# A delta-net decoder step on one core: the substitution on 16x16 blocks instead of 32x32

## The chip, the core and the metric

The kernel runs on one NeuronCore of a Trainium2 chip. Five engines work side by side, each through its own queue in order: TensorE (PE, matmuls), VectorE (DVE), ScalarE (ACT), GpSimd (POOL) and SyncE (SP), which here issues all DMAs. They wait for each other by semaphores. An engine that waits holds up everything behind it in its own queue. The metric is the device time of one execution in microseconds; below it is the median of several runs.

## The reference

Two layers, each with four mixers on the same normalised input; the change is in the first of them, the gated delta net. There are 272 prompt positions (16 learned ones and 256 tokens) and 8 sequences of 4 new tokens, 304 columns in all. The recurrence is computed in chunks, and each chunk needs a unit lower triangular system solved:

```python
def step(s, inp):
    qc, kc, vc, bc, gc = inp
    gcum = jnp.moveaxis(jnp.cumsum(gc, axis=1), 1, 2)
    decay = jnp.exp(jnp.where(incl, gcum[..., :, None] - gcum[..., None, :], -jnp.inf))
    kb = kc * bc[..., None]
    a = jnp.where(strict, jnp.einsum('bihk,bjhk->bhij', kb, kc) * decay, 0.0)
    rhs = jnp.concatenate([jnp.moveaxis(vc * bc[..., None], 1, 2),
                           jnp.moveaxis(kb, 1, 2) * jnp.exp(gcum)[..., None]], axis=-1)
    sol = lax.linalg.triangular_solve(a + eye, rhs, left_side=True, lower=True)
    u, w = sol[..., :dv], sol[..., dv:]
    v_new = u - jnp.einsum('bhik,bhkv->bhiv', w, s)
    ...
```

Around the mixers stand one input projection and one output projection per layer; these are most of the arithmetic:

```python
proj = jnp.einsum('bld,de->ble', rms_norm(x, lp['norm']), lp['w_in']).astype(f32)
...
y = x + jnp.einsum('ble,ed->bld', mixed.astype(x.dtype), lp['w_out'])
```

## The kernel before

**The main stream.** The loop at the end of `trunk` runs over units: layer, phase ("in" or "out"), output tile of 128 columns, and a quarter of the 2048 inputs. A unit is four weight blocks of 128x128 and three matmuls for each: the input as a high and a low part (`xh`, `xl`) against the weights' high part (`hi`), and the high input against the weights' low part (`lo`). Weights come by DMA into `raw`, ScalarE makes `hi`, VectorE makes `lo`, some units ahead of PE. This stream writes the tile `main` in PSUM (and `d` for the first units). In all there are 6144 of these matmuls in the order, 128x304 or a little narrower.

**The background threads.** The mixers are Python generators that a planner interleaves with the main stream while the program is built. After each weight block the loop calls `bg.poll()`; a thread gets its next stretch, up to its next `yield`, when the planner's clocks say that what it waits for is done by PE's clock. The clocks are kept in `Clocks.op`, with a price per operation in `price`. The resulting order is fixed when the program is built: each engine's queue is what the planner wrote. In each layer three thread groups run beside the in-phase: the delta net (`delta_thread`, one head pair after the other, PSUM tag `d`), a chain of row sums and the GLA pairs, and the RG-LRU and retention pairs (both tag `e`). The out-phase starts when all gated results (`m`) are there.

**The delta net's inverse.** For a pair of heads there are 2 heads and up to 10 diagonal blocks of 32x32 a head. `delta_thread` writes them to DRAM (`dk`), and reads them back so that a block lies in one partition's row: 20 blocks, four times over, on 80 partitions. Each copy r solves for 8 of the block's 32 right-hand columns. POOL then runs a forward substitution, one step per row j:

```python
for j in range(31):
    n, m = 31 - j, j // 4 + 1
    ...
    pool.tensor_mul(tv, bk[:, j:j + 1, j + 1:32].to_broadcast([80, m, n]), ...)
    pool.tensor_sub(xk[:, 0:m, j + 1:32], xk[:, 0:m, j + 1:32], tv)
```

The work tiles lie in the big buffers called `s9`. The inverses go through DRAM again (`dx`) into one tile `XB`; VectorE transposes it in blocks of 32, POOL copies the blocks into wide tiles `UF`, and PE joins 32 to 64 and 64 to 128 by small matmuls with the off-diagonal blocks of `BM` (the decayed k k^T). The results then solve for the chunk's values and states. In the profile the names `n`, `m` and `g` are shared work buffers, `hq` and `lq` are the high and low part of a square whose sum over partitions PE forms with `onesr`, `zk` and `zq` belong to the GLA pairs, `lso` to the RG-LRU, and `ssq` is the sum of squares for the norm. All of these calls go through one wrapper, so that the trace gives them one line, L298.

Of the kernel before, what the change touches and what calls it, by code (L numbers as in the profile page):

```python
# [17 lines left out]
L = 2  # L18
# [54 lines left out]
CSTU = 9  # L73
# [26 lines left out]
for _k, _w in (("id", 128), ("mask", 304), ("rm", 304), ("m8", 8), ("so", 96), ("st", 128), ("sm", 96), ("TS", 12), ("dec", 6), ("sgn", 1), ("hs", 2), ("m4", 4), ("um", 1), ("T4", 2)):  # L100
    CC[_k] = _n
    _n += _w
# [18 lines left out]
def constants():  # L121
# [3 lines left out]
    def put(name, a):  # L125
        c[:, CC[name]:CC[name] + a.shape[1]] = a
# [62 lines left out]
    put("sgn", sg)  # L189
    m4, um, T4 = np.zeros((128, 4), f), np.zeros((128, 1), f), np.zeros((128, 2), f)  # L190
# [14 lines left out]
class Clocks:  # L205
# [21 lines left out]
    def seen(self, table, k, kind="-"):  # L227
        end, by = table.get(k, (0.0, kind))
        return end if by == kind else end + 0.1
# [8 lines left out]
    def op(self, kind, cost, outs, ins):  # L238
        outs, ins = [self.key(x) for x in outs], [self.key(x) for x in ins]
        own = kind if kind not in "SG" else ""  # L240
        start = max([self.t[kind]] + [self.seen(self.wrote, k, own) for k in ins] +
# [108 lines left out]
def trunk(ctx: ExitStack, tc: tile.TileContext, I, O):  # L350
# [84 lines left out]
    xs_dram = dr.tile([128, KT, T], F32, name="xs_dram")  # L435
    scr_rows = [dr.tile([8, T], F32, name=f"rows{l}") for l in range(L)]
# [457 lines left out]
    def delta_thread(l, p, tag):  # L894
# [3 lines left out]
        dx = dr.tile([20, 1024], F32, tag="dx", name="dx", bufs=4)  # L898
# [82 lines left out]
        big = []  # L981
        for _ in range(2):
            big.append((yield from take9()))
        fl = [t.rearrange("p a b -> p (a b)") for t in big]
        bk = fl[0][0:80, :1024].rearrange("p (j i) -> p j i", i=32)
        xk = fl[1][0:80, :256].rearrange("p (m i) -> p m i", i=32)
        tk = fl[1][0:80, 256:512]
        for r in range(4):
            yield from put(fl[0][20 * r:20 * r + 20, :1024], dk)
        yield from put(fl[1][0:80, :256], I["xid"])  # L990
        yield from settled(*fl)
        for j in range(31):
            n, m = 31 - j, j // 4 + 1
            tv = tk[:, :n * m].rearrange("p (m i) -> p m i", m=m)
            pool.tensor_mul(tv, bk[:, j:j + 1, j + 1:32].to_broadcast([80, m, n]),
                            xk[:, 0:m, j:j + 1].to_broadcast([80, m, n]))
            pool.tensor_sub(xk[:, 0:m, j + 1:32], xk[:, 0:m, j + 1:32], tv)
            if j % 3 == 2:
                yield
        yield from settled(fl[1])  # L1000
        src = dx[0:20]
        for r in range(4):
            yield from put(bass.AP(tensor=src.tensor, offset=src.offset + 32 * r,
                                   ap=[[1024, 20], [128, 8], [1, 32]]), xk[20 * r:20 * r + 20])
        give9(*big)
# [20 lines left out]
        dve.transpose(out=XB[:, 192:384], in_=XB[:, 0:192])  # L1026
        for h in range(2):
            for a in range(4):
                nch = 3 if a < 2 else 2
                pool.tensor_copy(out=uf[h][32 * a:32 * a + 32, 0:nch, 32 * a:32 * a + 32],  # L1030
                                 in_=xb[32 * a:32 * a + 32, h, 0:nch, :])
            pool.tensor_copy(out=uf[h][0:48, 2, 64:128].rearrange("p (u s) -> p u s", u=2),
                             in_=uf[h][0:48, 2:3, 16:48].to_broadcast([48, 2, 32]))
# [598 lines left out]
    def begin(u):  # L1632
# [14 lines left out]
        if u == 6:  # L1647
            small_begin(0)
        if kt == KT:
            small_scale(0)  # L1650
            bg.add(level_masks())
# [113 lines left out]
def pack(i):  # L1765
# [38 lines left out]
    xid = np.zeros((4, 20, 8, 32), f)  # L1804
    for r in range(4):
        for m in range(8):
            xid[r, :, m, 4 * m + r] = 1
    d["xid"] = xid.reshape(80, 256)
# [40 lines left out]
```

## Time and profile before

| what | us |
|---|---|
| median of three runs | 1111.55 |
| lowest and highest run | 1108.95, 1111.94 |
| the profiled execution, whole | 1108.64 |
| its span, first to last instruction | 1106.8 |
| PE busy | 1051.6 |
| VectorE, ScalarE, POOL busy | 747.3, 634.1, 467.7 |

The mean granted clock of TensorE over the span is 0.98 of full speed. The trace is of one execution. A row of the timeline has the start in us from the span's start, the busy time, the engine, the operation with out<-in, the shape, the count, and in brackets the idle time before it with the instruction that ended it. A matmul in float32 appears as two records; the rows' counts are of records.

### The profile page before, as it was taken

To read this page: it belongs to the slowest core of one execution; us is meant where nothing else is said; L and a number is where in the kernel's file an instruction comes from. 1 tells how busy PE (TensorE), PEld (TensorE's weight loads), DVE (VectorE), ACT (ScalarE), POOL (GpSimd) and SP (SyncE) were. 2 spreads that over 40 slices of the span, in tenths; PEclk is the share of its full clock that TensorE was granted. 3 is DMA by queue.
4 is the path that set the end of the run, shared out by engine and by line. 5 is a ranking of instruction groups with operands and counts; after the bars stand their busy time and mean duration, and the time that the engine had idled before them with its cause. 6 is when DMAs were issued, how large, how long until landed. Compare 5 with 4: busy or idle time off the path is not lost.

```text
span 1106.8 us, 22879 instructions
## 1 busy us (share of the span) xinstructions
PE 1051.6 (95%) x7974; PEld 1000.7 (90%) x7974; DVE 747.3 (68%) x1449; ACT 634.1 (57%) x1430; POOL 467.7 (42%) x970
## 2 busy tenths in 40 slices
PE   8999989998999899999999999899899899999996
PEld 7899978988999889899999999789789799999995
DVE  5867579787566447666557756878975485666664
ACT  6677943665754356545455876456466347554442
POOL 4423378454426734222221348564434575431110
PEclk8999999999999979999999999899999999999998
DMA  6565435565467444666645555435564655556653
GB/s 208 174 163 173 145 104 162 152 197 179 129 214 227 125 135 152 197 198 217 205 135 154 170 167 154 126 112 166 151 195 136 211 175 165 188 184 208 195 185 142
DMA packets 116770, 187.47 MB, mean 169 GB/s; under 512 B 22144, under 2 KB 45168, under 8 KB 116656
## 3 DMA queue, kind: packets, MB, share of 16 engines
q1 hardware_dynamic: 116656, 186.03, 55.1%
q8 instruction: 62, 1.02, 0.4%
q14 instruction: 52, 0.43, 0.1%
HBM read 164.93 MB, written 19.80 MB: 167 GB/s over the span
## 4 chain that ended last, share of the span: by engine, by line
PE 63%; POOL 11%; DVE 10%; DMA 7%; ACT 4%; issue 4%; SPq 1%; DVEq 0%; ACTq 0%; POOLq 0%
PE main L298 51%; PE e L298 6%; DMA raw<-in_w_in_dram 5%; PE d L298 5%; POOL s9.4_168 L298 4%; DVE lo L298 3%; POOL s9.2_3662 L298 3%; DVE n L298 2%; POOL m L298 1%; SPq L298 1%; ACT hi L298 1%; ACT n L298 1%; DVE lq L298 1%; DVE zq L298 1%; POOL n L298 1%
## 5 line engine op out<-in xcount | busy, mean ns | idle before, releaser
L298 PE MATMUL main<-xh,hi 128*128 128x304 f32 (+2 forms) x1488 | 472.3, 317 | 4.6 <-ACT xh L298 3.2
L298 DVE TENSOR_TENSOR lo<-raw,hi 128x512 fp32r<-128x512 f32 (+1 forms) x513 | 399.1, 796 | 104.6 <-ACT hi L298 100.9
L298 PE MATMUL main<-xh,lo 128*128 128x304 f32 (+2 forms) x1488 | 453.2, 305 | 14.9 <-DVE lo L298 14.9
L298 ACT ACTIVATE hi<-raw 128x512 fp32r<-128x512 f32 (+1 forms) x513 | 316.9, 626 | 248.9 <-DMA raw<-in_w_in_dram 95.7
L298 PE MATMUL main<-xl,hi 128*128 128x304 f32 (+2 forms) x1488 | 450.6, 303 | 0.1
L298 PEld LDWEIGHTS main<-xh,lo 128*128 128x128 f32 x1488 | 284.2, 191 | 19.6 <-DVE lo L298 19.5
L298 PEld LDWEIGHTS main<-xh,hi 128*128 128x128 f32 x1488 | 284.5, 191 | 17.2 <-issue 7.4
L298 PEld LDWEIGHTS main<-xl,hi 128*128 128x128 f32 x1488 | 284.9, 191 | 2.5 <-DVE xl L298 0.8
L298 PE MATMUL main<-m,hi 128*128 128x304 f32 (+1 forms) x1024 | 208.8, 298 | 0.0
L298 PEld LDWEIGHTS main<-m,hi 128*128 128x128 f32 x1024 | 166.5, 188 | 0.0
L298 PE MATMUL main<-m,lo 128*128 128x304 f32 (+1 forms) x512 | 153.5, 300 | 0.0
L298 POOL TENSOR_TENSOR ssq<-ssq,n 128x304 f32<-128x304 f32 (+1 forms) x29 | 34.8, 1199 | 168.3 <-ACT n L298 168.3
L298 PEld LDWEIGHTS main<-m,lo 128*128 128x128 f32 x512 | 96.1, 188 | 0.5 <-DVE lo L298 0.5
L298 POOL COPY cvo<-ct 128x3 f32<-128x3 f32 x64 | 32.3, 534 | 117.4 <-DVE ct L298 117.3
L298 ACT ACTIVATE n<-n 128x304 f32<-128x304 f32 (+4 forms) x118 | 49.7, 439 | 43.2 <-DVE n L298 27.0
L298 POOL TENSOR_TENSOR n<-n,n 128x304 f32<-128x304 f32 (+1 forms) x39 | 37.3, 970 | 86.8 <-ACT n L298 56.1
L298 DVE TENSOR_TENSOR n<-main,n 128x304 f32<-128x304 f32 (+1 forms) x32 | 14.9, 466 | 60.3 <-PE main L298 50.8
L298 ACT ACTIVATE m<-m 128x304 f32<-128x304 f32 (+6 forms) x98 | 40.8, 433 | 11.9 <-DVE m L298 4.1
L298 DVE SCALAR_TENSOR_TENSOR acc<-ct,par,acc 128x328 f32<-128x328 f32 x64 | 41.9, 655 | 7.0 <-ACT acc L298 5.6
L365 ACT ACT_TABLE_LOAD x31 | 39.8, 1283 | 0.5
L298 ACT ACTIVATE n<-e 128x304 f32<-128x304 f32 (+5 forms) x66 | 19.7, 315 | 29.2 <-DVE n L298 15.7
L298 DVE TENSOR_TENSOR n<-main,rstd 128x304 f32<-128x304 f32 (+1 forms) x39 | 18.0, 462 | 24.5 <-PE main L298 24.3
(400 smaller groups left out, 1378.0 us busy)
## 6 DMA issues: line engine op xcount, KB each, us to landing
raw<-in_w_in_dram SPq DMA_DIRECT2D x383, 256.0 KB
raw<-in_w_out_dram SPq DMA_DIRECT2D x128, 256.0 KB
n<-o_dram SPq DMA_DIRECT2D x28, 152.0 KB
m<-in_x_dram SPq DMA_DIRECT2D x16, 152.0 KB
n<-in_x_dram SPq DMA_DIRECT2D x16, 152.0 KB
xs_dram<-n SPq DMA_DIRECT2D x16, 152.0 KB
n<-xs_dram SPq DMA_DIRECT2D x16, 152.0 KB
o_dram<-m SPq DMA_DIRECT2D x14, 152.0 KB
```

Source lines behind the costliest of these rows:

```text
L298: r = f(*a, **k)
L365: nc.scalar.preload_act_table_set(want[0])
```

## The change

The diagonal blocks are taken as 16x16. Each 32x32 block gives two of them, so 40 blocks, now twice over instead of four times on the 80 partitions; each copy solves for 8 of 16 columns, in 15 steps of two POOL operations. The inverses are written into `dx` at the place of the two diagonal quarters; the other two quarters have to be zero, so `dx` becomes four fixed DRAM tiles that are zeroed once, early in the program, from a work tile that POOL clears. `XB` then holds block-diagonal 32x32 tiles X. After the transpose, PE multiplies all 24 blocks (2 heads, 3 chunks, 4 row groups) by the 32x32 block of `BM` into one PSUM bank, ScalarE copies the product to `MS`, PE multiplies again by X, and VectorE adds the product, with a factor of -1 on partitions 0 to 15 of each 32 and 0 on the others (`hm`), to columns 16 to 31 of `XB`. A second transpose follows, and POOL's copies into `UF` stand behind it. For four of the 24 blocks' places, which hold no data, another block of `BM` is used, and the product is not used. The planner gets a lag of 0.12 us between a POOL operation and a POOL operation that reads its result.

```diff
--- before.py
+++ after.py
@@ -97,7 +97,7 @@
 
 CC = {}
 _n = 0
-for _k, _w in (("id", 128), ("mask", 304), ("rm", 304), ("m8", 8), ("so", 96), ("st", 128), ("sm", 96), ("TS", 12), ("dec", 6), ("sgn", 1), ("hs", 2), ("m4", 4), ("um", 1), ("T4", 2)):
+for _k, _w in (("id", 128), ("mask", 304), ("rm", 304), ("m8", 8), ("so", 96), ("st", 128), ("sm", 96), ("TS", 12), ("dec", 6), ("sgn", 1), ("hm", 1), ("hs", 2), ("m4", 4), ("um", 1), ("T4", 2)):
     CC[_k] = _n
     _n += _w
 NCST = _n
@@ -187,6 +187,9 @@
     sg[0:4] = 1
     sg[32:36] = -1
     put("sgn", sg)
+    hm = np.zeros((128, 1), f)
+    hm[np.arange(128) % 32 < 16] = -1
+    put("hm", hm)
     m4, um, T4 = np.zeros((128, 4), f), np.zeros((128, 1), f), np.zeros((128, 2), f)
     for j in range(128):
         t = j % 16
@@ -224,9 +227,9 @@
             return n, ap.offset % (KT * T) // T
         return (n, ap.offset) if n.split("_")[0] in SLICED else n
 
-    def seen(self, table, k, kind="-"):
+    def seen(self, table, k, kind="-", late=0.0):
         end, by = table.get(k, (0.0, kind))
-        return end if by == kind else end + 0.1
+        return end + late if by == kind else end + 0.1
 
     def free(self, ap):
         k = self.key(ap)
@@ -238,7 +241,8 @@
     def op(self, kind, cost, outs, ins):
         outs, ins = [self.key(x) for x in outs], [self.key(x) for x in ins]
         own = kind if kind not in "SG" else ""
-        start = max([self.t[kind]] + [self.seen(self.wrote, k, own) for k in ins] +
+        late = 0.12 if kind == "G" else 0.0
+        start = max([self.t[kind]] + [self.seen(self.wrote, k, kind if kind == "G" else own, late) for k in ins] +
                     [self.seen(self.wrote, k, kind) for k in outs if kind != "S" or self.wrote.get(k, "  ")[1] != "S"] +
                     [self.seen(self.read, k, own) for k in outs])
         if kind == "P" and cost < 0.2 and outs[0][:4] == "main" and self.last != "main":
@@ -433,6 +437,7 @@
 
     o_dram = dr.tile([128, KT, T], F32, name="o_dram")
     xs_dram = dr.tile([128, KT, T], F32, name="xs_dram")
+    dxs = [dr.tile([20, 1024], F32, name=f"dx{i}") for i in range(2 * L)]
     scr_rows = [dr.tile([8, T], F32, name=f"rows{l}") for l in range(L)]
 
 
@@ -895,7 +900,7 @@
         hs = (2 * p, 2 * p + 1)
         yield from need(("rows", l))
         dk = dr.tile([20, 1024], F32, tag="dk", name="dk", bufs=4)
-        dx = dr.tile([20, 1024], F32, tag="dx", name="dx", bufs=4)
+        dx = dxs[2 * l + p]
         K, Q, V, KN, VB, KTL, Eb, AT, qe, egl = ({} for _ in range(10))
         yield from need(*[("conv", l, k + h) for h in hs for k in (0, 4, 8)])
         GB = yield from take(2)
@@ -978,31 +983,33 @@
         yield from settled(dk)
 
         yield
-        big = []
-        for _ in range(2):
-            big.append((yield from take9()))
-        fl = [t.rearrange("p a b -> p (a b)") for t in big]
-        bk = fl[0][0:80, :1024].rearrange("p (j i) -> p j i", i=32)
-        xk = fl[1][0:80, :256].rearrange("p (m i) -> p m i", i=32)
-        tk = fl[1][0:80, 256:512]
-        for r in range(4):
-            yield from put(fl[0][20 * r:20 * r + 20, :1024], dk)
-        yield from put(fl[1][0:80, :256], I["xid"])
-        yield from settled(*fl)
-        for j in range(31):
-            n, m = 31 - j, j // 4 + 1
+        big = yield from take9()
+        fl = big.rearrange("p a b -> p (a b)")
+        bk = fl[0:80, :512].rearrange("p (j i) -> p j i", i=32)
+        xk = fl[0:80, 512:640].rearrange("p (m i) -> p m i", i=16)
+        tk = fl[0:80, 640:704]
+        for r in range(2):
+            for u in range(2):
+                n = 512 - 16 * u
+                yield from put(fl[40 * r + 20 * u:40 * r + 20 * u + 20, :n],
+                               bass.AP(tensor=dk.tensor, offset=dk.offset + 528 * u, ap=[[1024, 20], [1, n]]))
+        yield from put(fl[0:80, 512:640], I["xid"])
+        yield from settled(big)
+        for j in range(15):
+            n, m = 15 - j, j // 2 + 1
             tv = tk[:, :n * m].rearrange("p (m i) -> p m i", m=m)
-            pool.tensor_mul(tv, bk[:, j:j + 1, j + 1:32].to_broadcast([80, m, n]),
+            pool.tensor_mul(tv, bk[:, j:j + 1, j + 1:16].to_broadcast([80, m, n]),
                             xk[:, 0:m, j:j + 1].to_broadcast([80, m, n]))
-            pool.tensor_sub(xk[:, 0:m, j + 1:32], xk[:, 0:m, j + 1:32], tv)
-            if j % 3 == 2:
+            pool.tensor_sub(xk[:, 0:m, j + 1:16], xk[:, 0:m, j + 1:16], tv)
+            if j % 2:
                 yield
-        yield from settled(fl[1])
-        src = dx[0:20]
-        for r in range(4):
-            yield from put(bass.AP(tensor=src.tensor, offset=src.offset + 32 * r,
-                                   ap=[[1024, 20], [128, 8], [1, 32]]), xk[20 * r:20 * r + 20])
-        give9(*big)
+        yield from settled(big)
+        for r in range(2):
+            for u in range(2):
+                k = 40 * r + 20 * u
+                yield from put(bass.AP(tensor=dx.tensor, offset=dx.offset + 528 * u + 32 * r,
+                                       ap=[[1024, 20], [64, 8], [1, 16]]), xk[k:k + 20])
+        give9(big)
         XB = yield from take(1, True)
         pool.memset(XB[64:128, 0:192], 0.0)
         yield from settled(dx)
@@ -1024,6 +1031,26 @@
         uf = {h: UF[h].rearrange("p (c i) -> p c i", c=3) for h in range(2)}
         yield from settled(XB)
         dve.transpose(out=XB[:, 192:384], in_=XB[:, 0:192])
+
+        yield
+        hca = [(h, c, a) for h in range(2) for c in range(3) for a in range(4)]
+        hexa = lambda t: t[:, :192].rearrange("p (h c i) -> p h c i", h=2, c=3)
+        pa = pt(tag)
+        for h, c, a in hca:
+            r = slice(32 * a, 32 * a + 32)
+            k = 128 * c + 32 * a if c < 2 or a < 2 else 0
+            pe.matmul(hexa(pa)[r, h, c], BM[h][r, k:k + 32], xt[r, h, c], start=True, stop=True)
+        dx_ = hexa(MS)
+        activ(MS[:, 0:192], pa[:, 0:192], AF.Copy)
+        yield
+        pa = pt(tag)
+        for h, c, a in hca:
+            r = slice(32 * a, 32 * a + 32)
+            pe.matmul(hexa(pa)[r, h, c], dx_[r, h, c], xb[r, h, c], start=True, stop=True)
+        six = lambda t: t[:, 0:192].rearrange("p (k i) -> p k i", i=32)[:, :, 16:32]
+        dve.scalar_tensor_tensor(six(XB), six(pa), C("hm", 0), six(XB), op0=mul, op1=add)
+        dve.transpose(out=XB[:, 192:384], in_=XB[:, 0:192])
+        yield
         for h in range(2):
             for a in range(4):
                 nch = 3 if a < 2 else 2
@@ -1646,6 +1673,12 @@
             store(lst, I["s_lru"])
         if u == 6:
             small_begin(0)
+        if u == CSTU + 1:
+            z = S9s[-1][1].rearrange("p a b -> p (a b)")[0:20, 0:1024]
+            pool.memset(z, 0.0)
+            for x in dxs:
+                store(x, z)
+            S9s[-1][0] = clk.free(S9s[-1][1])
         if kt == KT:
             small_scale(0)
             bg.add(level_masks())
@@ -1801,11 +1834,11 @@
         put("dtb", l, i["dt_bias"][l][:, None])
     put("fn", None, i["final_norm"].reshape(16, 128).T)
     d["par"] = p
-    xid = np.zeros((4, 20, 8, 32), f)
-    for r in range(4):
+    xid = np.zeros((2, 40, 8, 16), f)
+    for r in range(2):
         for m in range(8):
-            xid[r, :, m, 4 * m + r] = 1
-    d["xid"] = xid.reshape(80, 256)
+            xid[r, :, m, 2 * m + r] = 1
+    d["xid"] = xid.reshape(80, 128)
     d["cst"], d["lev"], d["ret"] = constants()
     cb = np.concatenate([i["state_delta_conv"].reshape(L, 8, 3, 12, 128),
                          i["state_lru_conv"].reshape(L, 8, 3, 4, 128)], 3)
```

How the order moves, at three places. First POOL, at the start of the substitution of the first pair in layer 0 (`s9.4_168` and `s9.3_171` are the work tiles, `zk` belongs to a GLA pair, `m` here to the RG-LRU). Before:

```order
L298 TENSOR_TENSOR zk_91<-n_148,g_132 128x2x64
L298 TENSOR_TENSOR s9.4_168<-s9.3_167,s9.4_168 80x31
L298 TENSOR_TENSOR s9.4_168<-s9.4_168 80x31
L298 TENSOR_TENSOR s9.4_168<-s9.3_167,s9.4_168 80x30
L298 TENSOR_TENSOR s9.4_168<-s9.4_168 80x30
L298 TENSOR_TENSOR s9.4_168<-s9.3_167,s9.4_168 80x29
L298 TENSOR_TENSOR s9.4_168<-s9.4_168 80x29
L298 TENSOR_TENSOR m_619<-m_619,m_621 128x304
L298 TENSOR_TENSOR m_619<-m_619,m_602 128x8
L298 TENSOR_TENSOR m_615<-m_615,m_613 128x304
L298 TENSOR_TENSOR m_615<-m_615,m_599 128x8
L298 TENSOR_TENSOR s9.4_168<-s9.3_167,s9.4_168 80x28
```

The same place in the changed order:

```order
L302 TENSOR_TENSOR zk_91<-n_152,g_136 128x2x64
L302 TENSOR_TENSOR s9.3_171<-s9.3_171 80x15 x2
L302 TENSOR_TENSOR s9.3_171<-s9.3_171 80x14 x2
L302 TENSOR_TENSOR m_628<-m_628,m_630 128x304
L302 TENSOR_TENSOR m_628<-m_628,m_611 128x8
L302 TENSOR_TENSOR m_624<-m_624,m_622 128x304
L302 TENSOR_TENSOR m_624<-m_624,m_608 128x8
L302 TENSOR_TENSOR s9.3_171<-s9.3_171 80x26
L302 TENSOR_TENSOR s9.3_171<-s9.3_171 80x2x13
L302 TENSOR_TENSOR s9.3_171<-s9.3_171 80x24
```

After the first chunk and the four RG-LRU operations the substitution was at its fourth step of 31 and is at its third of 15; a stretch between two yields has four operations instead of six.

Second PE, at the first joining products of this pair (`g` and `n` are tiles of the delta thread). Before, the first batch was the one that joins 32 to 64:

```order
L298 MATMUL d<-g_138,g_128 32x32 x4
L298 MATMUL d<-g_138,g_129 32x32 x4
L298 MATMUL main<-xh,hi 128x304
L298 MATMUL main<-xl,hi 128x304
L298 MATMUL main<-xh,lo 128x304
```

In the changed order two batches of 24 come first; the batch above follows 33 projection matmuls behind the second of them:

```order
L302 MATMUL d<-g_142,g_132 32x32 x12
L302 MATMUL d<-g_142,g_133 32x32 x12
L302 MATMUL main<-xh,hi 128x304
L302 MATMUL main<-xl,hi 128x304
L302 MATMUL main<-xh,lo 128x304
...
L302 MATMUL d<-g_142,g_145 32x32 x24
L302 MATMUL e<-s9.2_170,lxg 32x128 x9
```

What moved: the new batches stand behind 978 and 984 projection matmuls of the program; the batch that joins 32 to 64 stood behind 1062 and stands behind 1017.

Third PE, at the end of layer 0's in-phase, where the output projection (`main<-m`) begins. Before, two state updates of the delta net (`s9`) stood in front of it:

```order
L298 MATMUL main<-xh,lo 128x304
L298 MATMUL d<-s9.4_6057,n_5645 128x512 x2
L298 MATMUL d<-s9.0_6076,n_5735 128x512 x2
L298 MATMUL main<-m_4118,hi 128x304
L298 MATMUL main<-m_4119,hi 128x304
L298 MATMUL main<-m_4118,lo 128x304
```

In the changed order nothing stands there; the last of these updates comes 96 projection matmuls earlier:

```order
L302 MATMUL main<-xh,hi 128x304
L302 MATMUL main<-xl,hi 128x304
L302 MATMUL main<-xh,lo 128x304
L302 MATMUL main<-m_4192,hi 128x304
L302 MATMUL main<-m_4193,hi 128x304
L302 MATMUL main<-m_4192,lo 128x304
```

Over the whole program the order has 192 matmuls more on PE, 127 operations fewer on POOL, 8 more on VectorE, 4 more on ScalarE, and 4 more DMAs.

## Rows read from the trace of the kernel before

**Rows 1.** Page, parts 1 and 2: busy us (share) xinstructions; clock in 40 slices, tenths.

```profile
PE 1051.6 (95%) x7974; PEld 1000.7 (90%) x7974; DVE 747.3 (68%) x1449; ACT 634.1 (57%) x1430; POOL 467.7 (42%) x970
PEclk8999999999999979999999999899999999999998
```

**Rows 2.** Windows: length, then PE, PEld, DVE, ACT, POOL busy (instructions), PEclk, DMA share, GB/s.

```profile
141.40:180.10 38.70, 34.63 (x263) 32.48 (x263) 31.53 (x81) 14.80 (x31) 34.12 (x86) 0.96 0.42 126
341.60:379.20 37.60, 34.06 (x240) 32.58 (x239) 23.99 (x43) 17.62 (x42) 33.17 (x88) 0.95 0.52 162
658.10:703.50 45.40, 40.12 (x278) 38.59 (x277) 29.39 (x56) 28.05 (x69) 37.76 (x100) 0.92 0.51 147
868.10:901.90 33.80, 28.84 (x201) 27.23 (x200) 20.70 (x28) 13.64 (x26) 29.39 (x75) 0.95 0.61 196
390.00:412.00 22.00, 19.81 (x144) 17.62 (x143) 8.81 (x16) 12.64 (x34) 8.09 (x22) 0.69 0.48 149
425.00:455.00 30.00, 27.22 (x206) 26.00 (x204) 22.90 (x34) 18.47 (x36) 11.79 (x10) 1.00 0.39 120
464.00:564.00 100.00, 99.97 (x717) 99.84 (x717) 61.16 (x92) 49.95 (x92) 20.09 (x15) 1.00 0.67 205
```

**Rows 3.** Timeline 146 to 150: start, us, engine, operation [idle before <-releaser].

```profile
148.14 0.56 DVE L298 TENSOR_TENSOR n<-m 128x136 f32<-128x136 f32 x2 [5.03 <-POOL zk L298]
149.44 0.41 PE L298 MATMUL main<-xh,lo 128*128 128x304 f32 x1 [2.41 <-DVE lo L298]
```

**Rows 4.** Groups of POOL, 141.4 to 180.1: out<-in xcount | busy us, mean ns | idle.

```profile
L298 POOL TENSOR_TENSOR s9.4_168<-s9.4_168 80x60 f32<-80x60 f32 (+24 forms) x31 | 13.2, 426 | 2.4
L298 POOL TENSOR_TENSOR s9.4_168<-s9.3_167,s9.4_168 80x60 f32<-80x60 f32 (+24 forms) x31 | 13.1, 423 | 3.3 <-DMA s9.4_168<-in_xid_dram 1.5
```

**Rows 5.** Timeline of POOL, first substitution step of the run.

```profile
141.44 0.24 POOL L298 TENSOR_TENSOR s9.4_168<-s9.3_167,s9.4_168 80x31 f32<-80x31 f32 x1 [1.50 <-DMA s9.4_168<-in_xid_dram]
141.76 0.25 POOL L298 TENSOR_TENSOR s9.4_168<-s9.4_168 80x31 f32<-80x31 f32 x1
```

**Rows 6.** Timeline of PE around two batches of 32x32 matmuls, first pair.

```profile
196.78 0.30 PE L298 MATMUL main<-xh,lo 128*128 128x304 f32 x1
197.01 0.44 PE L298 MATMUL d<-g,g 32*32 32x32 f32 x16
197.38 0.41 PE L298 MATMUL main<-xh,hi 128*128 128x304 f32 x1
197.63 0.30 PE L298 MATMUL main<-xl,hi 128*128 128x304 f32 x1
198.41 0.45 PE L298 MATMUL d<-g,g 32*32 32x32 f32 x24
198.79 0.41 PE L298 MATMUL main<-xh,hi 128*128 128x304 f32 x1
```

**Rows 7.** Timeline of DVE, the transpose of the joined inverses, first pair.

```profile
193.03 0.37 DVE L298 STREAM_TRANSPOSE g<-g 128x192 f32<-128x192 f32 x1
```

**Rows 8.** Timelines: the last ssq sum (POOL, PE), a POOL memset, four SP issues.

```profile
35.09 1.01 POOL L298 TENSOR_TENSOR ssq<-ssq,m 128x304 f32<-128x304 f32 x1 [0.61 <-ACT m L298]
36.15 0.78 PE L298 MATMUL e<-ssq,ones 128*128 128x304 f32 x2 [0.28 <-POOL ssq L298]
188.07 0.77 POOL L298 MEMSET g<- 128x384 f32 x2
187.50 2.12 SPq L298 DMA_DIRECT2D g<-dx  x4
```

**Rows 9.** Timeline of PE: 395 to 398, and the end of layer 0's in-phase.

```profile
395.34 0.40 PE L298 MATMUL e<-hq,onesr 128*128 128x304 f32 x1 [0.80 <-ACT hq L298]
397.13 0.62 PE L298 MATMUL e<-lq,onesr 128*128 128x304 f32 x1 [1.39 <-DVE lq L298]
453.32 0.50 PE L298 MATMUL d<-s9.0_6076,n 128*128 128x512 f32 x1 [1.33 <-DVE s9.2_3662 L298]
```

## The prediction

> **What bounds the kernel now.** First the busy shares: PE is busy 95% of the span, and its clock is at its upper level (2.4 GHz) but for a few slices [rows 1]. Then the steady stretch from 464 to 564 us, the output projection of layer 0: 717 matmuls keep PE busy for 99.97 of 100 us, 0.139 us apart [rows 2]. So the end is set by PE's own work, plus the time in which PE stands, plus the time in which it runs at the lower of its two levels (1.2 GHz, clock 0.50). Only the last two can be given back by this change: over the whole span PE is not busy for 1106.8 - 1051.6 = 55.2 us.
>
> Third, the windows in which POOL runs the delta net's substitution. There are four, one for each head pair of each layer; I found them as the stretches in which POOL works on 80 partitions, and put the third's end 5 us late to hold the clock's fall behind it. In them POOL is busy 83 to 88% of the time, PE is idle by 4.1, 3.5, 5.3 and 5.0 us and its clock is granted to 0.96, 0.95, 0.92 and 0.95 [rows 2]. A stretch of T us at clock c has done the work of cT, so the clock costs 1.5 + 1.9 + 3.6 + 1.7 = 8.7 us. Together the four windows lose 17.9 + 8.7 = 26.6 us in 155.5 us, 0.17 us for each us. The rest of the in-phases loses far less; the two stretches that I speak of apart are 390 to 412 (2.2 idle, and 6.8 by clock 0.69) and 425 to 455 (2.8 idle) [rows 2].
>
> How POOL reaches PE shows in the first window. VectorE stands 5.03 us for `zk`, a POOL product of another thread that is queued behind substitution steps; the next weight split (`lo`) stands behind that on VectorE, and PE stands 2.41 us for `lo` [rows 3]. It is a queue's delay, not a need for the inverse: nothing waits on that yet.
>
> **The substitution on POOL.** Before, each pair runs 31 steps of two operations, 62 in all, with 26.3 us busy in the first window (13.2 + 13.1) [rows 4]; the other windows are about as long [rows 2]. A bare step shows 0.24 us and the next start 0.32 us after [rows 5], so 0.08 us lies between dependent operations: 62 x 0.08 = 5.0 us more, some 31 us a pair. After, 15 steps, 30 operations, of 8 to 36 elements a row instead of 8 to 76. At the same mean of 26.3 / 62 = 0.42 us, plus 0.08, they take 15 us. POOL is relieved of 16 us a pair, some 64 us in all. None of this is itself on the path. What it buys is shorter windows: 15 us plus half of the 34.1 - 26.3 = 7.8 us of other threads' POOL work that now lies in the first window [rows 2, 4] makes 19 us, 76 us in all instead of 155.5. At the windows' own rate of loss 26.6 x 76 / 155.5 = 13.0 us remain, 13.6 go. The 79.5 us set free still lose at the rate of the rest: 55.2 idle and about 0.02 x 1106.8 = 22 by the clock, less the stretches named, leave 39 us in some 900, start and end included; 0.043 x 79.5 = 3.4 us comes back. Net gain 10.2 us. Its bounds: nothing (the delay lies with the other threads' work) to all 26.6.
>
> **The join on PE.** Each pair gets two batches of 24 matmuls of 32x32, 8 batches in all, 192 matmuls (the profile records each as two). No row shows four row groups at once. The nearest: 8 matmuls on two row groups (16 records) hold PE from 197.01 to 197.38, 0.37 us, and 12 on three (24 records) from 198.41 to 198.79, 0.38 us [rows 6]. The third group costs nothing, so time goes by records per group: 8 rounds in 0.38 us. A batch has 48 / 4 = 12 rounds: 0.57 us if four groups overlap as three do, 48 rounds or 2.28 us if they don't at all. I take the first, 8 x 0.57 = 4.6 us, since three groups overlap in full; bounds 3.0 us (the 0.38 of the existing batches) to 18.2. Leaving the projection for small matmuls has a toll too: the last start before is 0.23 us off instead of 0.14 and the first after 0.25, 0.2 us in all [rows 6]. Counted over both orders PE leaves the projection 240 times in each, so I add nothing; the bound is 8 x 0.2 = 1.6 us.
>
> The Trainium skill (TensorEngine Tiling (Array Packing), Gotcha 1: PSUM Pressure) speaks against that choice: different row tiles are to write to different PSUM banks and cannot use one bank at the same time. Here all four row groups write one bank, while the batches in the rows above have a bank for each. By that rule a batch is serial, and the eight cost 18.2 us rather than 4.6. No row of before has the case, so it is a rival below. What makes me doubt it is that here each group also writes its own 32 partitions.
>
> **The rest of the join.** ScalarE gets one copy of 192 columns a pair, VectorE one masked operation of 96 elements a partition and a second transpose (0.37 us in the row of the existing one [rows 7]). VectorE's masked operation waits for the second batch, and behind it stand the second transpose and the weight splits; PE waits for `lo` only when its lead of finished splits is used up. I cost these at nothing, because PE's projection runs beside them; the cover gone, and the masked operation taken to be as dear as the transpose, 4 x 2 x 0.37 = 3 us. POOL's copies of the inverse into the wide tiles move behind the second transpose.
>
> **The other DMAs and the start.** dk is read in four pieces of half the size, xid is halved, dx is written in pieces of 16. The counts are the same, and their SP slots too. New are a memset of 20x1024 on POOL ahead of the last `ssq` sum and four stores behind it on SP. The last sum starts at 35.09 after 0.61 us without work, and PE stands 0.28 us for it at 36.15 [rows 8]. By two memsets of 384 elements in 0.77 us [rows 8] one of 1024 takes 1.0 us, which fits the gap but for 0.4 us, and PE sees that: +0.4 us. Four issues take SP 2.12 us [rows 8] and hold back the weight loads queued behind them; the splits run ahead of PE there by up to three tiles of 12 matmuls, 5 us, so I take 0 for that, with 2.1 as upper bound.
>
> **The order.** With fewer steps, and 0.12 us of lag priced between dependent POOL operations (0.08 in the trace), the planner places the first joined product of the four pairs after 1017, 1890, 3852 and 4875 projection matmuls instead of 1062, 2064, 3972 and 4983. In layer 0 that is 174 x 0.139 = 24 us earlier for the second pair. Two losses sit there. At 394 us the join met another thread's sum of squares (PE waits 0.80 for `hq` and 1.39 for `lq` [rows 9]), the clock fell to its lower level, and the 22 us lost 9.0. It may go wholly or recur elsewhere; I take two thirds, 6.0. At the phase's end the last state update waits 1.33 us in front of the output projection [rows 9]; it now stands 96 matmuls earlier. I take 1.5 of the 2.8 us there.
>
> **Sum.** +4.6 + 0.4 - 10.2 - 6.0 - 1.5 = -12.7 us. The profiled execution took 1108.64 us (span 1106.8 and 1.8 around it), so 1095.9. The timed runs lie from 0.3 to 3.3 us above it, their median 2.9; I add 1.5 and say 1097.
>
> **Rivals.** (a) The row groups serialise, as the rule on banks has it: +13.6 us on the forecast, 1110.6, no change to speak of. For it: no batch before shares a bank. Against: the separate partitions. (b) The windows' loss moves on rather than going, since the other threads' POOL, VectorE and PE work is the same and only packed closer: then only the +5.0 remains, and the gain at 394 and at the end is lost too: 1108.64 + 1.5 + 5.0 = 1115. For it: the waits behind `lq` and `zk` outside the windows. Against: 0.17 us lost per us inside them, 0.04 outside. (c) Slower by a new wait: before, the first batch came 3.6 us after the transpose it needs (193.03 + 0.37 to 197.01 [rows 6, 7]), with POOL's ten copies in between; now it follows the transpose directly. If PE reaches it as much as 3.6 us early in each pair, and the clock falls as it did after the 2.41 us wait (1.5 us), this costs 4 x 5.1 = 20 us: 1117. It outweighs the gain of 12.7 from 3.2 us a pair. Against: before, the transpose itself found its data there and VectorE did not stand in front of it (the row is one of four alike [rows 7]), so the DMAs ahead of it are planned late enough. (d) More goes: all of the windows', the stretch's and the end's loss but what comes back: -26.6 - 9.0 - 2.8 + 3.4 + 5.0 = -30.0, 1080.
>
> **Chances.** Forecast 0.60, (a) 0.10, (b) 0.10, (c) 0.08, (d) 0.12. About 0.3% (3.3 us) is what a measurement of this kernel can tell from no change. Faster by more: the forecast, (d) and a tail of (a), 0.76. Within: most of (a) and the edge of (b), 0.10. Slower: (b) and (c), 0.14. The range runs from (d) at 1080 to just past (a), 1111, which leaves (b), (c) and the tails out; the forecast's own range is 1088 to 1106.
>
> **What would show it.** Right: 30 operations on 80 partitions a pair over 16 to 20 us; PE's idle time down by 8 to 15 us, with fewer stretches at 0.50; batches of 48 records in about 0.6 us; no wait at 453. Wrong: a batch of over 2 us (a); the same 55 us of idle time at other places (b); PE waiting for VectorE's transposed tile in front of the new batches (c); a hole or a low clock from 34 to 42 us, where the new stores are.

## The result, and the profile after

The changed kernel takes 1091.3 us (median of 4 runs, 1089.7 to 1094.1), beside 1111.7 us for the kernel before on the same chip: a ratio of 0.983 [0.981, 0.985]. Its profiled execution took 1089.9 us with a span of 1088.0, so 18.8 us less span than before. The forecast was 1097, range 1080 to 1111.

The page of the changed kernel, parts 1 and 2, against [rows 1]:

```profile
PE 1042.6 (96%) x8358; PEld 995.1 (91%) x8358; DVE 746.0 (69%) x1457; ACT 639.7 (59%) x1438; POOL 412.9 (38%) x843
PEclk9999999999999999999999999999999999999998
```

PE is not busy for 1088.0 - 1042.6 = 45.4 us, 9.8 less than before. The mean granted clock is 0.991 (before 0.980), so the clock costs 9.8 us instead of 22.1, 12.3 less. Together 22.1 us are given back, and the new matmuls take 4.4. The difference, 17.7, is nearly the 18.8 us of the spans; 1.1 us is not placed. The timed runs bear out the clock: 0.986 to 0.991 in all four, beside 0.972 to 0.985 in the later sessions' runs of the kernel before. POOL lost 54.8 us of work, and no slice of the clock's row but the last is under 9.

Next the stretches that answer to [rows 2], with the same columns. The first four run only as long as POOL works on 80 partitions; then the two single stretches of the forecast, taken 10 to 12 us earlier because the order has moved up; then a piece of the output projection:

```profile
140.30:161.20 20.90, 18.91 (x142) 16.92 (x141) 17.63 (x36) 9.98 (x24) 18.65 (x47) 1.00 0.30 99
327.10:347.60 20.50, 19.55 (x148) 19.02 (x146) 15.00 (x24) 11.89 (x29) 18.55 (x43) 1.00 0.65 216
645.60:658.50 12.90, 12.90 (x95) 12.90 (x94) 7.60 (x14) 11.49 (x24) 10.59 (x31) 1.00 0.44 144
836.30:851.60 15.30, 15.30 (x114) 14.88 (x113) 9.91 (x19) 7.82 (x14) 13.08 (x32) 1.00 0.65 211
380.00:402.00 22.00, 22.00 (x187) 20.81 (x186) 14.23 (x30) 13.81 (x34) 12.10 (x24) 1.00 0.52 170
413.00:443.00 30.00, 28.57 (x202) 28.15 (x202) 21.64 (x30) 18.66 (x32) 9.37 (x7) 1.00 0.62 199
450.00:550.00 100.00, 100.00 (x720) 100.00 (x719) 60.17 (x90) 48.56 (x90) 18.85 (x14) 1.00 0.65 206
```

The steady matmuls have the speed of before; the last two windows lose nothing at all, and PE is busy without a break from 366 to 412 us, in the stretch that stood at 394. But short windows flatter the change, because waits can come just behind them. So the same view for what follows each window, until the four have about their length of before (157.8 us with the 69.6 above; before 155.5):

```profile
161.20:180.10 18.90, 16.93 (x141) 15.61 (x140) 17.49 (x58) 6.43 (x15) 7.80 (x26) 1.00 0.52 152
347.60:366.00 18.40, 17.33 (x225) 15.57 (x226) 10.29 (x22) 8.06 (x22) 11.38 (x30) 1.00 0.49 139
658.50:690.90 32.40, 29.66 (x354) 27.11 (x353) 23.56 (x57) 21.35 (x66) 20.45 (x50) 1.00 0.58 174
851.60:870.10 18.50, 18.01 (x134) 17.50 (x132) 8.97 (x16) 8.31 (x14) 3.34 (x6) 1.00 0.68 210
```

Idle time of PE is 2.9 us in the windows and 6.3 us behind them, 9.2 in all, where 17.9 stood before. The clock, which cost 8.7 us there, is at 1.00 in all eight rows.

PE at the first of the four joins (start, us, engine, operation), which answers to [rows 6]:

```profile
179.85 0.30 PE L302 MATMUL main<-xh,lo 128*128 128x304 f32 x1
180.18 0.62 PE L302 MATMUL d<-g,g 32*32 32x32 f32 x48
180.72 0.41 PE L302 MATMUL main<-xh,hi 128*128 128x304 f32 x1
...
181.89 0.62 PE L302 MATMUL d<-g,g 32*32 32x32 f32 x48
```

From a batch's first start to the next matmul it is 0.55 us, the same in all eight batches: 4.4 us.

Some waits are left or new. PE around four of them (in brackets the idle time and what ended it):

```profile
247.08 0.52 PE L302 MATMUL e<-zq,zk 128*64 128x64 f32 x10 [2.74 <-DVE zq L302]
247.53 0.41 PE L302 MATMUL main<-xh,hi 128*128 128x304 f32 x1
247.77 0.30 PE L302 MATMUL main<-xl,hi 128*128 128x304 f32 x1
247.91 0.30 PE L302 MATMUL main<-xh,lo 128*128 128x304 f32 x1
...
673.27 0.62 PE L302 MATMUL d<-g,g 32*32 32x32 f32 x48 [1.79 <-ACT g L302]
...
746.61 0.50 PE L302 MATMUL d<-s9.1_10128,m 128*128 128x512 f32 x1 [2.18 <-DVE s9.2_3655 L302]
...
747.36 0.30 PE L302 MATMUL main<-xh,hi 128*128 128x292 f32 x1
747.50 0.29 PE L302 MATMUL main<-xl,hi 128*128 128x292 f32 x1
...
748.47 0.45 PE L302 MATMUL main<-xh,hi 128*128 128x292 f32 x1
748.71 0.44 PE L302 MATMUL main<-xl,hi 128*128 128x292 f32 x1
...
939.32 0.62 PE L302 MATMUL d<-lq,onesr 128*128 128x304 f32 x1 [3.03 <-DVE lq L302]
939.74 0.44 PE L302 MATMUL main<-xh,hi 128*128 128x288 f32 x1
939.98 0.44 PE L302 MATMUL main<-xl,hi 128*128 128x288 f32 x1
```

Behind the last two, projection matmuls start 0.24 us apart instead of 0.14: the clock has fallen to its lower level, for 3.4 us each time (granted 0.50, from 747.7 and from 938.8), as it did in the kernel before around the waits at 149 and 395 to 397. Behind the first, of 2.74 us, it has not: the matmuls go on 0.14 us apart.

### The profile page after: what moved, and what is told of

Same layout as the page of the kernel before. It is cut to its first block, busy times and chain, and to the rows that moved or that the text cites. A ratio compares the mean times of both kernels' runs of the same rounds, so it can differ in the third digit from the quotient of the medians.

```text
span 1088.0 us, 23535 instructions
## 1 busy us (share of the span) xinstructions
PE 1042.6 (96%) x8358; PEld 995.1 (91%) x8358; DVE 746.0 (69%) x1457; ACT 639.7 (59%) x1438; POOL 412.9 (38%) x843
## 4 chain that ended last, share of the span: by engine, by line
PE 67%; DVE 13%; DMA 5%; POOL 5%; issue 5%; ACT 4%; SPq 1%; DVEq 0%; ACTq 0%; POOLq 0%
PE main L302 55%; PE e L302 6%; PE d L302 5%; DMA raw<-in_w_in_dram 4%; DVE lo L302 4%; DVE m L302 2%; DVE n L302 2%; POOL m L302 2%; ACT hi L302 1%; DVE zq L302 1%; DVE acc L302 1%; POOL s9.4_4198 L302 1%; POOL n L302 1%; ACT L369 1%; SPq L302 1%
## 5 line engine op out<-in xcount | busy, mean ns | idle before, releaser
L302 DVE TENSOR_TENSOR lo<-raw,hi 128x512 fp32r<-128x512 f32 (+1 forms) x513 | 391.7, 782 | 101.6 <-ACT hi L302 100.0
L302 ACT ACTIVATE m<-m 128x304 f32<-128x304 f32 (+5 forms) x95 | 39.3, 431 | 6.9 <-DVE m L302 3.1
```

The source lines that it names most:

```text
L302: r = f(*a, **k)
```

## The experiments

Theory A, the forecast's: what counts is the length of POOL's queue; fewer operations in it let the products that others wait for come sooner. Its rivals: it is the new order (B), or POOL's work costs by contending with VectorE. Each run is set beside the kernel before in the same session (medians of before 1109.8 to 1110.8).

**1. The lag alone, in the kernel before.** The planner prices 0.12 us between dependent POOL operations; nothing else changes.

```diff
-        return end if by == kind else end + 0.1
+        return end + late if by == kind else end + 0.1
...
+        late = 0.12 if kind == "G" else 0.0
-        start = max([self.t[kind]] + [self.seen(self.wrote, k, own) for k in ins] +
+        start = max([self.t[kind]] + [self.seen(self.wrote, k, kind if kind == "G" else own, late) for k in ins] +
```

> The kernel before with one part of the change alone: the 0.12 us lag that the planner adds between dependent POOL operations. Theory A (the gain of the change comes from POOL's shorter queue in the four substitution windows): the queue is as long as before, so 1103 to 1115 us, and the windows of 33 to 40 us still lose 15 us or more in PE idle time and clock. Theory B (the gain comes from the order that the planner writes with its better price): 1098 us or less.

Measured: 1118.4, ratio 1.008 [1.006, 1.010]. That is slower than either theory had it, so the lag brings no part of the gain. The four windows (41, 37, 44 and 33 us, the third 5 us longer as in [rows 2]) show why they must not be read alone:

```profile
141.00:182.40 41.40, 37.74 (x279) 34.63 (x277) 33.63 (x84) 15.74 (x33) 36.03 (x89) 0.96 0.42 128
352.80:389.90 37.10, 35.20 (x260) 33.91 (x260) 19.90 (x39) 20.10 (x48) 32.59 (x83) 0.95 0.50 159
663.40:707.60 44.20, 40.78 (x285) 39.53 (x285) 27.63 (x51) 26.93 (x64) 37.77 (x100) 0.96 0.43 127
867.40:900.40 33.00, 31.61 (x233) 30.48 (x232) 18.59 (x33) 16.44 (x29) 28.25 (x67) 1.00 0.72 223
...
444.00:464.00 20.00, 14.59 (x71) 13.49 (x70) 10.12 (x14) 7.46 (x15) 6.40 (x5) 0.74 0.40 130
```

They lose 10.4 by idling and 5.3 by the clock, 15.7 instead of 26.6, with the same POOL work. But the loss reappears elsewhere, above all at the end of layer 0 (last row): PE waits 1.89 and 3.37 us, the clock drops to 0.74, and 20 us lose 10.6. A new order alone moved the time by some 8 us here.

**2. The changed kernel without the lag.** The two lines with `late` in `op` taken back.

> The changed kernel with the planner of before, without the 0.12 us lag. Theory A: POOL's queue is as short as in the changed kernel, so 1088 to 1098 us. Theory B: the order is planned with the old price, so most of the gain goes, 1104 us or more.

Measured: 1091.9, ratio 0.984 [0.981, 0.987]. That cannot be told from the changed kernel; the lag is worth nothing there either.

**3. The relief alone, in the order of before.** The planner still counts all 31 steps, but POOL issues only the first 15 (`ghost` is an engine that the planner counts and that issues nothing), and there is no join: the inverses stay incomplete.

```diff
+            p_ = pool if j < 15 else ghost
-            pool.tensor_mul(tv, ...
-            pool.tensor_sub(xk[:, 0:m, j + 1:32], ...
+            p_.tensor_mul(tv, ...
+            p_.tensor_sub(xk[:, 0:m, j + 1:32], ...
```

> The kernel before with its order kept on every engine, but POOL leaves out the steps 15 to 30 of the 31 of the substitution (the planner still counts them, the inverses are not complete). No join is added. Theory A: POOL's queue is half as long, so the windows' loss goes and nothing is paid for the join: 1082 to 1095 us. Theory B: the order is that of before, so 1106 to 1112 us.

Measured: 1091.3, ratio 0.983 [0.979, 0.986]: as much as the whole change, without any new order. It has no join to pay for, and yet is no faster than the changed kernel; whether the new order gives those 4 us back, or the intervals of some 3.5 us to either side hide them, is open. The trace is of the fastest of its four runs, 5.7 us below their median, so it flatters the relief. The windows, at the places and lengths of [rows 2], and the stretch that stood at 390, with its two waits, here 6 us earlier:

```profile
141.20:179.90 38.70, 34.83 (x265) 32.55 (x264) 31.20 (x81) 15.00 (x32) 23.86 (x57) 0.96 0.44 130
341.00:378.50 37.50, 36.85 (x286) 35.62 (x285) 25.20 (x47) 19.45 (x45) 26.40 (x58) 1.00 0.58 183
647.20:692.60 45.40, 45.21 (x347) 43.84 (x346) 33.26 (x75) 31.63 (x77) 33.84 (x81) 1.00 0.58 169
849.00:882.80 33.80, 31.23 (x231) 29.53 (x230) 19.44 (x32) 16.22 (x32) 21.68 (x55) 1.00 0.70 220
...
384.00:406.00 22.00, 19.82 (x184) 17.98 (x183) 12.39 (x23) 15.85 (x41) 7.13 (x22) 1.00 0.57 173
...
389.39 0.40 PE L298 MATMUL e<-hq,onesr 128*128 128x304 f32 x1 [0.80 <-ACT hq L298]
390.90 0.41 PE L298 MATMUL e<-lq,onesr 128*128 128x304 f32 x1 [1.11 <-DVE lq L298]
```

In the four windows PE loses 7.3 us by idling and 1.5 by the clock: 8.8 instead of 26.6. The first window keeps its loss (5.4) and the fourth 2.6 us of 6.7. The first window's is the very wait of [rows 3]:

```profile
148.01 0.56 DVE L298 TENSOR_TENSOR n<-m 128x136 f32<-128x136 f32 x2 [5.34 <-POOL zk L298]
...
149.31 0.41 PE L298 MATMUL main<-xh,lo 128*128 128x304 f32 x1 [2.67 <-DVE lo L298]
```

It comes 7 us into the window, when POOL has only done early steps, of which both kernels have as many. Later in a pair the shorter queue tells.

**4. The work put back, in the changed order.** Behind each step POOL gets more products, 32 a pair, that the planner doesn't know of; one more memset a pair clears the scratch part that they work on.

```diff
+        nc.gpsimd.memset(fl[0:80, 704:1088], 0.0)
...
+            w = fl[0:80, 704:1088]
+            for _ in range(2 if j else 4):
+                nc.gpsimd.tensor_mul(w[:, 0:60], w[:, 0:60], w[:, 64:124])
```

> The changed kernel with its order kept on every engine, but with 32 further POOL operations of 80x60 per head pair behind the steps of the substitution, which the planner does not know of. They work on a scratch part of the tile, and the output does not depend on them. That makes 62 operations per pair, as before. Theory A: the windows grow to 35 us or more, and the waits behind them come back: 1100 to 1125 us. Theory B: POOL's load hardly counts, 1089 to 1094 us.

Measured: 1127.8, ratio 1.017 [1.015, 1.019]: the gain is gone and 17 us more, 3 us above theory A's range. Only the first two windows grow past 35 us (to 40 and 52; the others take 27 and 31). PE in the third and fourth pair, and POOL behind the third pair's steps:

```profile
695.45 1.27 PE L302 MATMUL e<-cst,n 128*128 128x2 f32 x6 [10.16 <-POOL n L302]
...
877.50 0.80 PE L302 MATMUL e<-s9.1_11624,n 128*128 128x512 f32 x1 [4.98 <-POOL s9.1_11624 L302]
```

```profile
690.66 3.48 POOL L302 TENSOR_TENSOR m<-m,m 128x304 f32<-128x304 f32 x5
694.10 1.30 POOL L302 TENSOR_TENSOR n<-g,m 128x304 f32<-128x304 f32 x1
```

Another thread's `n` stands in POOL's queue behind the steps, and PE waits 10.2 us for it; in the changed kernel it waits 0.95 us. The order had placed PE's use of it for the short queue.

**5. Half of that work.** 16 products a pair.

```diff
+            for _ in range(1 if j else 2):
```

> The refill with half as many products, 16 per pair, unknown to the planner, in the order of the changed kernel. If the loss grows evenly with POOL's load: midway between the changed kernel (1091) and the full refill (1128), 1104 to 1114 us. If the order has room for some lateness on POOL and only what exceeds it costs: 1091 to 1100 us.

Measured: 1104.4, ratio 0.996 [0.993, 0.998]: 13 us above the changed kernel, where the full load costs 36. That is the lower edge of the first range. POOL's busy time grows by 19.8 us here and by 42.0 with the full load, so 47% of the work cost 36% of the time. The cost rises with the load; whether it rises faster than in proportion is not shown, because each of these medians is uncertain by 2 to 3 us.

**6. The same load as memsets.** 32 a pair, of 80x400, instead of the products.

```diff
+            for _ in range(2 if j else 4):
+                nc.gpsimd.memset(fl[0:80, 704:1104], 0.0)
```

> As the run with the refilled substitution, but the 32 further POOL operations per pair are memsets of 400 columns, which read nothing and take about 0.45 us each, unknown to the planner; the order is that of the changed kernel. If POOL hurts by its queue (other threads' operations stand behind it): 1105 to 1130 us, like the refill with products. If it hurts by slowing VectorE's operations that run at the same time, through reads of both: much less, 1092 to 1103 us.

Measured: 1130.2, ratio 1.018 [1.015, 1.020], at the upper edge of the first range, and PE waits 10.59 us for `n` at 695.9. Operations that read nothing cost as much, so it is the queue and not contention over operands. VectorE's own times say the same: a weight split (`lo`) takes 0.78 us in the mean in the changed kernel and in both of these runs.

**7. The same load, known to the planner.** As 4, but through the planner's wrapper.

```diff
+                pool.tensor_mul(w[:, 0:60], w[:, 0:60], w[:, 64:124])
```

> The refill with 32 products per pair, but now the planner knows of these operations and writes its order with them, as it did for the 62 operations of the kernel before. If the load on POOL itself costs the time: 1106 to 1122 us, which is the kernel before plus the join. If the refills hurt mainly because the order did not know of them: 1090 to 1102 us.

Measured: 1100.5, ratio 0.993 [0.990, 0.995]: 9 us above the changed kernel, but 27 under the unplanned load. In the trace 7.8 of the 9.7 us of longer span are the clock's (mean 0.984), 1.9 are idle time. Its four windows:

```profile
132.50:183.60 51.10, 48.70 (x355) 46.34 (x353) 39.52 (x101) 24.18 (x55) 38.83 (x101) 0.93 0.44 137
330.30:371.60 41.30, 40.60 (x315) 38.98 (x314) 24.81 (x47) 24.50 (x56) 32.45 (x85) 1.00 0.57 181
643.30:680.40 37.10, 37.10 (x268) 36.66 (x267) 22.05 (x37) 29.00 (x66) 33.41 (x90) 1.00 0.50 159
840.00:883.00 43.00, 42.28 (x314) 40.78 (x313) 24.89 (x41) 20.73 (x39) 28.41 (x71) 1.00 0.63 188
```

POOL is busy 133 of 172 us, yet PE loses only 3.8 by idling and 3.6 by the clock. A busy POOL alone does not cost what it cost before; it costs where PE's order asks for a product earlier than the queue gives it.

**8. The join's batches issued twice**, without the planner knowing.

```diff
+        for h, c, a in hca:
...
+            nc.tensor.matmul(hexa(pa)[r, h, c], BM[h][r, k:k + 32], xt[r, h, c], start=True, stop=True)
...
+        for h, c, a in hca:
...
+            nc.tensor.matmul(hexa(pa)[r, h, c], dx_[r, h, c], xb[r, h, c], start=True, stop=True)
```

> The changed kernel with its order kept, but PE issues each of the 8 join batches of 24 matmuls twice, which the planner does not know of; the result is the same. Theory A (PE's own work sets the end, and the batches lie on the path at 0.55 us each, as the trace of the changed kernel shows): 8 x 0.55 = 4.4 us more, 1094 to 1098 us. Rival (PE's small matmuls fit into time in which PE waits anyway): no more than 1 us on the changed kernel, 1089 to 1093 us.

Measured: 1096.0, ratio 0.986 [0.984, 0.989], 4.7 us above the changed kernel. The intervals of the two overlap; the trace is sharper. Seven of the eight doubled batches of 96 records last 0.95 us; one has a hole of 1.67 us in it, for which the trace names no cause. So 24 more matmuls take 0.40 us.

The trace also shows the wait for `zq` that stands at 247 in the changed kernel, here with the clock's fall behind it (0.51 from 251.8 to 255.2, matmuls 0.25 us apart):

```profile
251.75 0.77 PE L302 MATMUL e<-zq,zk 128*64 128x64 f32 x10 [2.73 <-DVE zq L302]
...
252.87 0.46 PE L302 MATMUL main<-xl,hi 128*128 128x304 f32 x1
253.12 0.46 PE L302 MATMUL main<-xh,lo 128*128 128x304 f32 x1
```

**9 and 10. Remaining waits planned away.** Before PE's sum of squares, the thread yields until the planner has `lq` done; in the last run also before three other uses.

```diff
+        yield from settled(lo)
         ps = pt(tag)
         pe.matmul(ps[:, :T], onesr, hi, start=True, stop=False)
```

> The changed kernel, where a thread asks the planner that the low part `lq` is done, with its slack, before it puts the two matmuls of a sum of squares into PE's queue. PE waits about 8 us for `lq` in the changed kernel, and its two later falls of the clock follow such waits. Theory A (such waits are PE's own lost time): 1081 to 1089 us. Rival (the order moves elsewhere and loses as much): 1089 to 1096 us.

> As the run with the settled sums; the same question is asked of the planner before the GLA products of `zq` and `zk`, before the second batch of the join and before the second of two state updates. Theory A: these waits go too, 1076 to 1088 us. Rival: threads that yield more often finish later and the order loses elsewhere, 1088 to 1100 us.

Measured: 1091.7, 0.982 [0.979, 0.985], and 1093.6, 0.984 [0.982, 0.987]. No gain, and the traces show that the loss moves. PE's waits for `lq` fall from 6.7 us (the expectation's 8 is too high, and only the later of the two falls follows such a wait) to 3.4 and 0.9, but those for `lo` rise from 5.4 to 10.7 and 9.5. In the first of the two, idle time falls by 3.8 us and the clock costs 4.4 more. None of the variants beats the changed kernel.

## Why the prediction was right, and where it was not

**Direction and mechanism** were right, and the time lies in the range, 5.7 us below the forecast: the span fell by 18.8 us, where the forecast's sum has 12.7. The substitution has its 30 operations a pair, but over 20.8, 20.4, 12.8 and 15.3 us, where 16 to 20 were forecast; in the first window (groups of POOL, against [rows 4]):

```profile
L302 POOL TENSOR_TENSOR s9.3_171<-s9.3_171 80x30 f32<-80x30 f32 (+10 forms) x30 | 10.7, 356 | 1.8
```

**The join, +4.6.** Measured 4.4 in the trace. Four row groups overlap, each with its own 32 output partitions, and rival (a) is refuted for this placement. That the number fits is partly luck. The 12 matmuls of [rows 6] stand on two row groups and not on three (partitions 32 to 63 twice, with different output partitions, and 96 to 127). And the price per round was too high: in experiment 8 twelve more rounds take 0.40 us and not 0.57, so a part of the 0.55 is a price per batch, which the sum did not have. By the Trainium skill (TensorEngine Tiling (Array Packing), Gotcha 1: PSUM Pressure) different row tiles cannot use one PSUM bank at the same time, and a batch would be serial, an estimated 2.28 us by the rows of before; it takes 0.55 us with one bank written by all four row groups, so here the measurement decides against the rule. Rival (c) hardly happened: in front of the four first batches the last starts are 0.33, 0.67, 0.23 and 0.22 us off, and PE stands for the transposed tile 0.37 us in the second pair and almost nothing in the others. One second batch waits, 1.79 us for ScalarE's copy, which I had costed at nothing; ScalarE itself stood 2.27 us for a POOL memset queued behind four operations of another thread.

**The start, +0.4.** The memset takes 0.95 us (1.0 was estimated) and PE waits for the last `ssq` 0.50 us instead of 0.28: +0.2. The issues behind it on SP leave no hole.

```profile
34.26 0.95 POOL L302 MEMSET s9.4_172<- 20x1024 f32 x1
...
36.05 0.78 PE L302 MATMUL e<-ssq,ones 128*128 128x304 f32 x2 [0.50 <-POOL ssq L302]
```

**The windows, -10.2: the step that was mis-sized.** I let 13.0 us remain in 76 us of window, at the windows' own rate of loss. The 69.6 us of window lose 2.9. A rate fits them badly. My reading is that a delay grows along the queue, and that with half the steps most delays stay below what PE's lead of finished splits covers. This is not shown: the lead was not varied, and the bend in experiment 5 is too slight to prove it. Against that, 6.3 us appear right behind the windows. Over stretches of about equal length the loss goes from 26.6 to 9.2, a gain of 17.4, half of it (8.7) the clock. Why the clock held is not shown: its falls come with waits, but not with each, and no run changed the clock alone. One and the same wait can go either way: that of 2.74 us at 247 has no fall behind it here, but in experiment 8 (2.73 us, at 251.8) it has one.

**The stretch at 394, -6.0.** All 9.0 went. In the order of before with relief alone (experiment 3) the two waits are still there, 0.80 and 1.11 us, and PE idles 2.2 us in the 22 as before, but the clock stays at 1.00: with the load gone the old order gets 6.8 of the 9.0 back. So in these traces most of this term goes with the load and not, as I had it, with the earlier join.

**The end of layer 0, -1.5.** 2.8 us became 1.4. Right in size; the state updates at the phase's end no longer wait, and what is left is a wait for `lq` at 419.6.

**What comes back, +3.4** (counted in the windows' term). By place: -17.4 - 9.0 - 1.4 + 0.2 + 4.4 = -23.2, beside -18.8 measured: 4.4 us came back in the rest, not far from 3.4, with the two new waits at 744 and 936 and their clock's falls above (8.1 us from 743.9 and from 935.9 lose 5.5 together by idling and 3.4 by the clock). A clock fall at the start, 3.4 us long instead of 6.8, favours the change by 1.7 us and is luck: in experiment 3, with the order of before, it lasts 3.4 us, and in experiment 8, with the changed order, 6.8. Without it 6.1 us came back.

**Still open.** Before and experiment 7 carry about the same POOL work (467.7 and 467.4 us), the latter also the join, and yet it is 9 us faster. Experiment 1 shows that a new order alone can move the time by 8 us, so 9 us can be that; which of the two orders is the unlucky one, and whether a planner with better prices would find the good one, was not tried. So the load's share of the gain is not settled: taking it away in the old order gave some 19 us, putting it back with an order planned for it cost 9.

## What to carry to other kernels

Where an idle-looking helper engine serves several threads through one queue, price an edit there by whose results stand behind it, and how far the consumer's order leads; busy share and length of the window said little here, and a rate of loss per microsecond understated the shorter queue. Compare the loss over equal stretches of work, the windows and what follows them, and check the whole span too: an order that clears one stretch can lose it at another. To tell load from order, leave the work out, or add it, behind the planner's back.

## What the runs showed of the hardware

- 24 matmuls of 32x32 in four row groups, all to one PSUM bank, each group with its own 32 partitions of it, take 0.55 us from their first start to the next matmul's, and 24 more only 0.40 us; the batches of 12 over three pairs of row group and output partitions, with as many banks, take 0.38 us, in the kernel before and the changed one.
- A POOL memset of 80x400 takes 0.43 us, in all 128 of them; the products of 80x60 that it replaced take 0.40 us in the mean, from 0.31 to 0.87. PE's longest wait is 10.59 us with the one and 10.16 with the other.
- The granted clock fell to its lower level around PE's waits of 2.18 and 3.03 us, and not around one of 2.74 us at 247 us, which in experiment 8 had a fall behind it: the length of the one wait before it does not tell.
